# Hybrid attention and convolution layer on one core: key and value projections moved into the query projection's rounds

## The chip, the cores and the metric

The kernel is one launch on one core of a Trainium2 chip. The metric is the device time of that launch in microseconds (us), as a median over runs; lower is better. The core has five engines with their own instruction streams: TensorE (PE, matrix products into the accumulation memory PSUM), VectorE (DVE), ScalarE (ACT), GpSimd (POOL) and SyncE (SP). Here SP issues nearly all transfers; a few small ones are issued by POOL and ACT. Streams run in order, and wait for each other by semaphores.

## The reference

One layer of a diffusion backbone runs over two sets of tokens with the same weights: 128 context tokens and 512 latent tokens, width 1024, float32. Cut to what matters:

```
mod = silu(cond) @ w_ada + b_ada          # shift, scale, gate, twice
h   = rms(x) * norm * (1 + sc1) + sh1
q, k, v, gb, gc, u = split(h @ w_in)      # 512, 128, 128, 512, 512, 512 columns
q = rms_per_head(q); k = rms_per_head(k)  # 8 query heads, 2 key heads, 64 wide
latent q, k get a 2-D rotary position; context q, k do not
attn   = softmax(q k^T / 8) v             # latent: cached keys + latent keys
y_conv = gb * conv3(gc * u)
x = x + g1 * (concat(rms(attn), rms(y_conv)) @ w_out)
x = x + g2 * ((silu(gate) * up) @ w_down) # gate, up from a second normed h
```

The outputs are both sets of tokens after the layer, and the context's keys and values.

## The kernel before

Every matrix product that must be accurate is made of three products of a rounded number type (`mm3`): both operands are split into a rounded high part and the low rest (`split`: ACT copies with rounding, DVE subtracts), and high·high, high·low and low·high are added in PSUM. Tokens stand in five tiles of 128: latent tiles 0 to 3 and the context tile 4 (`CTX`). The contraction over the width of 1024 goes in eight blocks k of 128.

**The first stage** makes h and the query projection. For each k a piece of `w_ada` (two tiles `af` of 512 KB, two transfers each, L323) is multiplied with silu(cond) by `ada1_mm` (step `a`, L379), folded by `ada1_mod` (step `m`, L428) and turned into a scale and a shift by three small DVE operations (L402 to L406). `h_do` (step `h`) applies these to the transposed tokens `xT` and splits the result into `hH[k]` and `hL[k]`. Then five `q_mm` (digits) add block k of the query projection for the five token tiles, three products of 512 columns each, into five PSUM banks that stay open over all eight k. `P1PRE` and `P1SEQ` are written orders of these steps for k = 0 and for the rounds k = 1 to 7. In the first, `r` is a token tile's norm, `x` its transposes, `w` a weight split, `p` and `v` small loads and turns, `c` constants. Under `manual_schedule` PE follows the text's order throughout; DVE, ACT and POOL follow it in `P1PRE` only, and beyond it a scheduler of the framework chooses. `LOADS` is the order in which SP issues the first transfers. The `af` tiles have four buffers and the raw weights `wf` three, so SP waits for their release; split weights `wh` and `wl` have four buffers each.

**The second stage** begins with five evictions of the query projection to SBUF (`qraw`, L549 and L551, tile name `of`), the two transfers of the rotary tables (`act.dma_start`, L561 and L562, issued by ACT), and eight POOL operations on them that make the tables `tab` (L568 and L574). It then follows the written order `SEQ`. Here `k`t is `kv_mm` (L629): 24 products of 256 columns for the keys and values of tile t, then the per-head norm, rotary product and split of the keys (`head_norm`, `k_split`) and the store of the values. `c`/`C` do the same to the cached keys; `K`t turns keys by PE (`k_turn`, L621) and evicts them (L623, L624). `q`t norms and splits a query tile and `Q`t turns it (L657). `a`, `t`, `o` are the three steps of the context's own attention. `S`, `T`, `O` are the scores, transposes and output products of the sixteen latent units (two heads each; `S0.0` is the first). `F1` is a filler: the next third of one half of a convolution's product (`conv_mm`, L677 to L679, 24 products of 320 columns per half) or a piece of the later modulation (`ada_all`). There are 84 fillers (`NFILL`).

The inverse square roots of all norms are POOL operations (`rstd_of`, L164). The third stage (output projection) and the fourth (the FFN) take over half of the time and aren't touched.

Of the kernel before, what the change touches and what calls it, by code (L numbers as in the profile page):

```python
# [9 lines left out]
F32 = mybir.dt.float32  # L10
# [5 lines left out]
P = 128  # L16
# [16 lines left out]
SOQ = [0, -300, -300, -300]  # L33
# [3 lines left out]
XTE = [0, 1, 0, 1, 1, 1, 0, 1, 1, 0]  # L37
SEQ = ('k1 c0 q4 k4 C0 k0 K4 Q4 q0 a0 F1 k2 a1 K0 t0 k3 t1 o0 K1 F1 Q0 o1 K2 F1 K3 F1 S0.0 F1 F1 S0.1 '
# [48 lines left out]
LOADS = [0, 0, 0, 0, 2, 1, -1, 0, 3, 3, 2, 2]  # L87
# [3 lines left out]
def build(ctx, tc, x_prompt, x_sample, c, cache_k, cache_v, c_ctx, norm_mix, norm_ffn, w_ada, b_ada,  # L91
# [144 lines left out]
    def load_split(e, wf):  # L236
# [4 lines left out]
        if gain is None:  # L241
            with early(SOQ[key[1]] if key[0] == 'q' else SOW):
                split(wh, wl, wf)
# [108 lines left out]

    for a in LOADS:
        if a > 0:
            ada1_next(a)
        elif a < 0:
            load_next(True)
        else:
            x_load()
# [53 lines left out]
    def ada1_mm(k):  # L413
# [3 lines left out]
        for h, wf in enumerate(ada1[k]):  # L417
            for i in range(4):
                cond_mm(rp, 4 * h + i, wf[:, i].rearrange("p a b -> p (a b)"))
        res = T("res", (P, 256), F32, 2)  # L420
        dve.tensor_copy(res, rp)
        ada1[k] = res

    def ada1_mod(k):
        res = ada1.pop(k)
        mp = PB((P, 2, 1, 2))
# [5 lines left out]

    def xT_do(t):

        both = PS2() if t < XB else None
        tps = [both[:, i] if t < XB else PB() for i in range(2)]

        def turn(k):
            pe.transpose(tps[k // 4][:, k % 4 * P:(k % 4 + 1) * P], xs[t][:, k * P:(k + 1) * P], ident)

        if t < XB:
            for k in range(KD):
                turn(k)
        for i, tp in enumerate(tps):
            if t >= XB:
                for k in range(4):
                    turn(4 * i + k)
            dst, src = xT[:, 4 * i:4 * i + 4, t * P:(t + 1) * P], tp.rearrange("p (k q) -> p k q", q=P)
            if XTE[2 * t + i] == 0:
                act.activation(dst, src, AF.Copy)  # L450
            else:
                dve.tensor_copy(dst, src)
# [871 lines left out]
```

## Time and profile before

| what | value |
|---|---|
| median of 3 runs | 760.23 us (760.18 to 761.4) |
| the profiled execution's own time | 762.66 us |
| its span, first to last instruction | 760.9 us |
| granted TensorE clock, mean | 0.993 |
| PE busy (modelled ends) | 739.5 us, 97% |
| DVE busy | 552.7 us, 73% |
| ACT busy | 369.6 us, 49% |
| POOL busy | 43.1 us, 6% |
| first query-projection product to last | 20.46 to 65 us |
| first score products of the latent attention | 95.08 us |

In a timeline the first number is an instruction's start in us from the span's start, the second the time that it took; a matrix product's duration includes its way through the array, so that what one costs in a row of many is the distance of two starts. An idle time in square brackets is that of the engine before the instruction, with what ended it. "PEclk" is the granted share of the TensorE clock.

### The profile page before, as it was taken

The numbers are of one execution on the slowest core, as the hardware profiler recorded it, in microseconds if no ns is written. First come the engines' busy times: TensorE is split into PE (matmuls) and PEld (weight loads), VectorE is DVE, ScalarE is ACT, GpSimd is POOL, SyncE is SP. The second block draws the span as 40 slices with busy tenths as digits, with TensorE's granted clock in tenths as the row PEclk, the third lists the DMA queues.
The fourth block names the chain that finished last, engine by engine and source line by source line (L and its number), as shares of the span: only waits on it lengthen the run. The fifth ranks groups of instructions, "written<-read, shape, count | busy, mean of one in ns | idle before, by whom it ended". The sixth has DMA issues, their size and how long they took to land.

```text
span 760.9 us, 11844 instructions
## 1 busy us (share of the span) xinstructions
PE 739.5 (97%) x4580; PEld 664.6 (87%) x4580; DVE 552.7 (73%) x1003; ACT 369.6 (49%) x715; POOL 43.1 (6%) x73
## 2 busy tenths in 40 slices
PE   4999999999999999999999999999999999999997
PEld 3768888989998887899898789998889998899986
DVE  5556987676666797779879678884578866788653
ACT  5345867666656444765552135553125541255410
POOL 3104301011010110100000000000000000000000
PEclk9899999999999999999999999999999999999999
DMA  9985132522433363031335223223113132222312
GB/s 289 293 233 158 38 118 91 173 91 91 160 104 93 130 249 111 1 112 56 86 111 179 83 62 103 79 89 113 53 56 110 58 112 67 73 86 82 111 56 84
DMA packets 102349, 84.52 MB, mean 111 GB/s; under 512 B 4526, under 2 KB 82674, under 8 KB 102292
## 3 DMA queue, kind: packets, MB, share of 16 engines
q1 hardware_dynamic: 100980, 83.39, 35.5%
q8 instruction: 36, 0.59, 0.3%
q10 hardware_dynamic: 1056, 0.26, 0.2%
q0 software_dynamic: 256, 0.11, 0.1%
q14 instruction: 21, 0.17, 0.1%
HBM read 79.68 MB, written 2.75 MB: 108 GB/s over the span
## 4 chain that ended last, share of the span: by engine, by line
PE 82%; DVE 8%; DMA 3%; ACT 2%; SPq 2%; issue 1%; POOL 1%; DVEq 0%; POOLq 0%
PE pf L154 17%; PE pf L156 16%; PE pf L155 16%; PE pc L677 3%; PE pc L678 3%; PE pc L679 3%; PE po L834 3%; PE ps L791 2%; PE ph L154 2%; PE pt L817 2%; PE ph L155 2%; PE ph L156 2%; PE pc L379 2%; DMA af<-in_w_ada_dram 2%; DMA wf<-in_w_gate_up_dram 1%
## 5 line engine op out<-in xcount | busy, mean ns | idle before, releaser
L150 ACT ACTIVATE wh<-wf 128x1024 fp32r<-128x1024 f32 (+1 forms) x76 | 64.1, 843 | 95.7 <-PE pf L156 61.8
L154 PE MATMUL pf<-wh,gT 128*128 128x512 f32 (+1 forms) x225 | 88.1, 392 | 0.0
L155 PE MATMUL pf<-wl,gT 128*128 128x512 f32 (+1 forms) x225 | 87.7, 390 | 0.0
L156 PE MATMUL pf<-wh,gT 128*128 128x512 f32 (+1 forms) x225 | 87.7, 390 | 0.0
L151 DVE TENSOR_TENSOR wl<-wf,wh 128x1024 fp32r<-128x1024 f32 (+1 forms) x42 | 49.4, 1175 | 29.1 <-ACT wh L150 26.3
L677 PE MATMUL pc<-hH,wh 128*128 128x320 f32 x192 | 61.1, 318 | 0.0
L678 PE MATMUL pc<-hL,wh 128*128 128x320 f32 x192 | 59.4, 310 | 0.0
L679 PE MATMUL pc<-hH,wl 128*128 128x320 f32 x192 | 59.4, 309 | 0.0
L155 PEld LDWEIGHTS pf<-wl,gT 128*128 128x128 f32 x225 | 42.2, 188 | 10.0 <-issue 0.2
L154 PEld LDWEIGHTS pf<-wh,gT 128*128 128x128 f32 x225 | 42.2, 188 | 9.9 <-ACT wh L150 0.2
L156 PEld LDWEIGHTS pf<-wh,gT 128*128 128x128 f32 x225 | 42.2, 188 | 9.8
L154 PE MATMUL pf<-T,wh 128*128 128x320 f32 x160 | 49.7, 311 | 0.5 <-ACT u L1154 0.5
L155 PE MATMUL pf<-T,wl 128*128 128x320 f32 x160 | 49.5, 309 | 0.0
L155 PE MATMUL pf<-T,wh 128*128 128x320 f32 x160 | 49.5, 309 | 0.0
L156 PE MATMUL pf<-T,wh 128*128 128x320 f32 x160 | 49.5, 309 | 0.0
L154 PE MATMUL pf<-T,wl 128*128 128x320 f32 x160 | 49.5, 309 | 0.0
L156 PE MATMUL pf<-T,wl 128*128 128x320 f32 x160 | 49.5, 309 | 0.0
L154 PE MATMUL pf<-B,wl 128*128 128x320 f32 x152 | 47.3, 311 | 0.1
L156 PE MATMUL pf<-B,wl 128*128 128x320 f32 x152 | 47.1, 310 | 0.0
L155 PE MATMUL pf<-B,wl 128*128 128x320 f32 x152 | 47.0, 309 | 0.0
L1233 DVE TENSOR_TENSOR dm<-pf,g 128x512 f32<-128x512 f32 (+1 forms) x41 | 27.7, 675 | 22.8 <-PE pf L156 22.6
L154 PE MATMUL pf<-B,wh 128*128 128x320 f32 x136 | 42.3, 311 | 1.5 <-DVE cu L1183 1.5
(293 smaller groups left out, 2023.9 us busy)
## 6 DMA issues: line engine op xcount, KB each, us to landing
wf<-in_w_gate_up_dram SPq DMA_DIRECT2D x44, 512.0 KB, 4.0
aw<-in_w_ada_dram SPq DMA_DIRECT2D x24, 512.0 KB, 4.7
wf<-in_w_down_dram SPq DMA_DIRECT2D x20, 512.0 KB, 3.4
wf<-in_w_in_dram SPq DMA_DIRECT2D x18, 512.0 KB, 6.1
af<-in_w_ada_dram SPq DMA_DIRECT2D x32, 256.0 KB, 6.0
x<-in_x_sample_dram SPq DMA_DIRECT2D x8, 512.0 KB, 4.8
wf<-in_w_out_dram SPq DMA_DIRECT2D x8, 512.0 KB, 3.9
wf<-in_w_ada_dram SPq DMA_DIRECT2D x8, 512.0 KB, 3.7
```

The source lines that it names most:

```text
L150: act.activation(hi, src, AF.Copy)
L151: dve.tensor_tensor(lo, src, f32(hi), ALU.subtract)
L154: pe.matmul(out, lh, rh, start=start, stop=False, skip_group_check=more)
L155: pe.matmul(out, lh, rl, start=False, stop=False, skip_group_check=more)
L156: pe.matmul(out, ll, rh, start=False, stop=stop, skip_group_check=more)
L379: pe.matmul(out[CG * g:CG * (g + 1)], cp[:, k], w, start=(k < 4), stop=(k >= KD - 4), skip_group_check=True)
L677: pe.matmul(acc, wh[:, k], hH[k][:, c0:c0 + n], start=(k == 0), stop=False)
L678: pe.matmul(acc, wh[:, k], hL[k][:, c0:c0 + n], start=False, stop=False)
L679: pe.matmul(acc, wl[:, k], hH[k][:, c0:c0 + n], start=False, stop=(k == KD - 1))
L791: pe.matmul(s2[:, g, :320], q, kk[:, v, P + g * 320:P + (g + 1) * 320], start=(i == 0), stop=(i == 1))
L834: pe.matmul(ov, w, x[:, i].rearrange("p a q -> p (a q)"), start=(g == 0 and i == 0 and n == 0), stop=(last and i == len(kts) - 1 and n == 1))
L1233: dve.tensor_tensor(dm, ps[:, :n], g2[cc][:, oc], ALU.mult)
```

## The change

1. **Keys and values in the rounds.** `kv_mm` is gone. A new step `k` in the first stage (`kv_q`) does block k of the keys and values for the four latent tiles, two token tiles side by side in one PSUM bank, so that two banks stay open over the rounds; the first product into a bank starts it and only the last one ends it. A step `K` (`kv_ctx`) does all eight blocks for the context tile. The three results are evicted to SBUF (`kvctx`, `kvraw`), and the second stage's `k` (`kv_norm`) does only what followed the products.
2. **Loads.** The weights of keys and values are planned between those of the queries, and `LOADS` names all transfers of the stage: `x` a token tile, `A` one k of `w_ada`, `W` the next weights.
3. **Written orders.** One `P1SEQ` covers all rounds, and DVE, ACT, POOL and SP follow the text's order through it as PE does. The steps are cut finer: `r`/`s` (norm and scale), `e` (an eviction of transposes, with its engine), `a`/`b` (products and eviction of the modulation), `w`/`l` (high and low part of a weight). For k = 0 the latent part of h is made without the detour over `hF` on ACT.
4. **Idle products.** `spin` (step `d`) multiplies the identity with itself into a bank that nobody reads: 8, 2 and 4 times.
5. **Second stage.** `SEQ` begins with `k4` and has more fillers ahead of `S0.0` (11 where there were 4) and one fewer in six places behind it; 85 are listed, of which 84 exist as before. The modulation's small PSUM tiles now use the other tag, with one bank left for them beside the context's query sums.

```
-LOADS = [0, 0, 0, 0, 2, 1, -1, 0, 3, 3, 2, 2]
+LOADS = 'xxxxAWxAAWAWAWAWAWAW'
-P1SEQ = 'm h a 0 1 2 3 4'
-P1PRE = ('r0 r1 r2 x0 r3 x1 v0 x2 a0 w0 x3 m0 r4 h00 a1 q02 q01 x4 q00 m1 h01 h10 a2 q03 h11 p0 q04 c0')
+P1SEQ = ('d8 r0 s0 x0 r1 s1 r2 x1 e00d s2 e01d r3 v0 d2 x2 s3 a0 e10d e20a b0 x3 e11d e21a e30a m0 d4 w l h00y q02 r4 q01 e31d s4 '
+         'p0 a1 b1 x4 e40d m1 h01x h10 a2 q00 b2 q03 h11 q04 w l m2 e41a h20 h21 q10 q11 q12 a3 b3 q13 q14 '
+         'm3 h30 h31 q20 q21 w l c0 q22 q23 a4 b4 q24 k0 k1 m4 h40 h41 q30 q31 w l v1 q32 a5 b5 q33 q34 k2 k3 '
+         'm5 h50 h51 q40 q41 w l q42 a6 b6 q43 q44 k4 m6 h60 h61 q50 q51 w l q52 a7 b7 q53 q54 k5 '
+         'm7 h70 h71 q60 q61 q62 q63 q64 k6 K w l k7 q70 q71 q72 q73 q74')
-SEQ = ('k1 c0 q4 k4 C0 k0 K4 Q4 q0 a0 F1 k2 a1 K0 t0 k3 t1 o0 K1 F1 Q0 o1 K2 F1 K3 F1 S0.0 F1 F1 S0.1 '
+SEQ = ('k4 c0 F1 k0 q4 F1 C0 k1 F1 K4 F1 Q4 q0 a0 F1 k2 a1 F1 K0 t0 F1 k3 t1 o0 F1 K1 F1 Q0 o1 K2 F1 K3 F1 '
+       'S0.0 F1 F1 S0.1 q1 F1 F1 S1.0 F1 T0.0 S1.1 T0.1 T0.2 O0.0 F1 O0.1 O0.2 S2.0 T1.0 F1 T1.1 T1.2 S2.1 '
...
-    for j in range(4):
-        plan(("q", j), wi[:, 2 * j:2 * j + 2, O_Q:O_Q + 512])
-    for h in range(2):
-        plan(("kv", h), wi[:, 4 * h:4 * h + 4, O_K:O_K + 256])
+    for x in ("q", 0), ("q", 1), ("kv", 0), ("q", 2), ("kv", 1), ("q", 3):
+        n, o, w = (2, O_Q, 512) if x[0] == "q" else (4, O_K, 256)
+        plan(x, wi[:, n * x[1]:n * x[1] + n, o:o + w])
...
+    pe_order = tc.manual_schedule(engines={mybir.EngineType.PE})
+    pe_order.__enter__()
+    pre_order = tc.manual_schedule(engines={mybir.EngineType.DVE, mybir.EngineType.Activation, mybir.EngineType.Pool,
+                                            mybir.EngineType.SP})
+    pre_order.__enter__()
...
+        if alone and cc == 0:
+            act.activation(hH[k][:, s], xT[:, k, s], AF.Identity, bias=b, scale=a)
+            dve.tensor_scalar(hF[k][:, s], xT[:, k, s], a, b, ALU.mult, ALU.add)
+            dve.tensor_tensor(hL[k][:, s], hF[k][:, s], f32(hH[k][:, s]), ALU.subtract)
+            return
...
+    def spin(n):
+
+        for _ in range(n):
+            pe.matmul(qacc[-1][:, :P], ident, ident, start=True, stop=True)
...
+    def w_hi(_):
+        e, wf = deferred.pop(0)
+        a, b = e[1].shape[1], e[1].shape[2]
+        e[5] = T("wh", (P, a, b), F32R, WHB), T("wl", (P, a, b), F32R, WHB)
+        act.activation(e[5][0], wf, AF.Copy)
+        rounded.append((wf, *e[5]))
...
+    def kv_ctx():
+
+        kvacc.append(PB((P, 256), tag="c"))
+        for k in range(KD):
+            wh, wl = W(("kv", k // 4))
+            mm3(kvacc[2], hH[k][:, 512:TOK], hL[k][:, 512:TOK], wh[:, k % 4], wl[:, k % 4], k == 0, k == KD - 1)
+
+    def kv_q(k):
+
+        if not kvacc:
+            kvacc.extend(PB() for _ in range(2))
+        wh, wl = W(("kv", k // 4))
+        for t in range(NL):
+            s = slice(t * P, (t + 1) * P)
+            out = kvacc[t // 2][:, t % 2 * 256:t % 2 * 256 + 256]
+            first, last = ends("kv%d" % t)
+            mm3(out, hH[k][:, s], hL[k][:, s], wh[:, k % 4], wl[:, k % 4], first and t % 2 == 0, last and t % 2 == 1, True)
...
-    for k in range(1, KD):
-        ada1_next(3)
...
+    kvraw, kvctx = T("g1", (P, 2, 512), F32, 2), T("g1", (P, 256), F32, 2)
+    act.activation(kvctx, kvacc[2], AF.Copy)
+    act.activation(kvraw[:, 0], kvacc[0], AF.Copy)
+    dve.tensor_copy(kvraw[:, 1], kvacc[1])
...
-    def kv_mm(t):
-        acc = PB((P, 256), tag="c")
-        s = slice(t * P, (t + 1) * P)
-        for k in range(KD):
-            wh, wl = W(("kv", k // 4))
-            mm3(acc, hH[k][:, s], hL[k][:, s], wh[:, k % 4], wl[:, k % 4], k == 0, k == KD - 1)
+    def kv_norm(t):
+        acc = kvctx if t == CTX else kvraw[:, t // 2, t % 2 * 256:t % 2 * 256 + 256]
```

More of the change, by code (lines that the diff above doesn't have):

```diff
@@ L241, in load_split @@
         if gain is None:
-            with early(SOQ[key[1]] if key[0] == 'q' else SOW):
+            with early(SOW):
                 split(wh, wl, wf)
@@ L431, in build, with xT_evict, h_do @@
     xT = T("xT", (P, KD, TOK))
+    xps = {}
     def xT_do(t):
         both = PS2() if t < XB else None
[L436 to L441, printed above, removed]
-            for k in range(KD):
[L443 to L452, printed above, removed]
+        xps[t] = [both[:, i] if t < XB else PB() for i in range(2)]
+        for k in range(KD):
+            pe.transpose(xps[t][k // 4][:, k % 4 * P:(k % 4 + 1) * P], xs[t][:, k * P:(k + 1) * P], ident)
+    def xT_evict(t, i, e):
+        dst, src = xT[:, 4 * i:4 * i + 4, t * P:(t + 1) * P], xps[t][i].rearrange("p (k q) -> p k q", q=P)
+        if e == "a":
+            act.activation(dst, src, AF.Copy)
+        else:
+            dve.tensor_copy(dst, src)
     hF = {}
-    def h_do(k, cc):
+    def h_do(k, cc, alone):
         if k not in hF:
@@ L464, in h_do @@
             dve.tensor_scalar(hF[k][:, s], xT[:, k, s], a, b, ALU.mult, ALU.add)
-        if k == 0:
+        if alone:
             split(hH[k][:, s], hL[k][:, s], hF[k][:, s])
@@ L510, in rows2_load @@
         pool.dma_start(rows2[8:20, :], conv_w[0].rearrange("w (r q) -> (w r) q", q=P))
[L512 to L514 removed]
+    steps = {"r": x_norm, "s": x_scale, "c": late_consts, "w": w_hi, "l": w_lo, "p": lambda i: rows2_load(), "x": xT_do,
+             "v": lambda i: (vec_do, vec2_do)[i](), "m": ada1_mod, "a": ada1_mm, "b": ada1_res, "d": spin,
+             "k": kv_q, "K": lambda i: kv_ctx()}
     in_pre[0] = True
[L516 to L517 removed]
+    for x in P1SEQ.split():
+        k = int(x[1:2] or 0)
         if x[0] == "h":
[L519 removed]
+            h_do(k, int(x[2]), len(x) > 3)
         elif x[0] == "q":
             q_mm(k, int(x[2]))
+        elif x[0] == "e":
+            xT_evict(k, int(x[2]), x[3])
         else:
```

63 lines of the change are left out of this document (27 added, 36 removed), and 19 rows, old and new, of the table SEQ.

## The prediction

> **What bounds the kernel now.** I read the windows by stage first, then PE's timeline at the seams, then DVE, ACT and POOL between the two stages. Columns of the windows: busy time and instructions of PE, its weight loads, DVE, ACT, POOL; granted clock; DMA share; GB/s.
>
> ```profile
> 20.00:25.00 5.00, 5.00 (x23) 3.85 (x16) 1.12 (x3) 0.00 (x0) 1.38 (x3) 0.51 1.16 284
> 45.20:65.00 19.80, 19.80 (x115) 15.41 (x115) 9.05 (x21) 7.43 (x10) 1.42 (x2) 1.00 0.75 210
> 65.00:97.00 32.00, 29.81 (x235) 28.06 (x235) 28.43 (x85) 24.38 (x67) 12.57 (x20) 1.00 0.21 64
> 97.00:262.00 165.00, 164.25 (x1183) 148.31 (x1182) 116.05 (x229) 106.85 (x217) 13.91 (x24) 1.00 0.37 118
> 262.00:761.00 499.00, 492.86 (x2844) 449.24 (x2842) 375.35 (x605) 209.04 (x391) 6.74 (x7) 1.00 0.29 92
> ```
>
> From 97 us on PE is full and DVE at 70%: there an instruction taken from PE is time gained, as long as the softmax still finds its cover. From 65 to 97 us DVE is busy 28.4 of 32 us: the norms and splits of keys and queries set the pace, and PE is filled beside them. Before 65 us transfers, waits and a half clock rule. So the products of keys and values leave a stage that DVE bounds, for one in which PE has room.
>
> ```profile
> 12.62 1.16 PE L379 MATMUL pc<-af,cp 128*32 128x256 f32 x16
> 13.72 1.09 PE L439 MATMUL pt<-ident,x 128*128 128x128 f32 x8
> 20.46 0.79 PE L154 MATMUL ps<-wh,hH 128*128 128x512 f32 x1
> 41.57 0.75 PE L379 MATMUL pc<-af,cp 128*32 128x256 f32 x8 [1.52 <-DMA af<-in_w_ada_dram]
> 47.27 0.50 PE L428 MATMUL pt<-sel,res 128*128 128x2 f32 x4
> 47.70 1.07 PE L379 MATMUL pc<-af,cp 128*32 128x256 f32 x16
> 48.70 0.50 PE L154 MATMUL ps<-wh,hH 128*128 128x512 f32 x1
> 52.31 0.50 PE L428 MATMUL pt<-sel,res 128*128 128x2 f32 x4
> 57.35 0.50 PE L428 MATMUL pt<-sel,res 128*128 128x2 f32 x4
> 64.82 0.28 PE L154 MATMUL pc<-wh,hH 128*128 128x256 f32 x1
> 64.94 0.28 PE L155 MATMUL pc<-wl,hH 128*128 128x256 f32 x1
> 78.45 0.31 PE L677 MATMUL pc<-hH,wh 128*128 128x320 f32 x1
> 78.59 0.31 PE L678 MATMUL pc<-hL,wh 128*128 128x320 f32 x1
> 95.08 0.46 PE L791 MATMUL ps<-KA,qT 128*128 128x320 f32 x2
> 129.62 1.72 PE pc L739 x4
> ```
>
> By distance of starts: a `q` round is 52.31 - 48.70 = 3.6 us, `a` 1.0, `m` 0.43, a key product 0.12, a filler product 0.147.
>
> **Rounds, PE.** Five token tiles times 24 products at 0.12 are 14.3 us, now issued before the stage's end. From `a0` at 12.62 on PE has to issue 8 x (3.6 + 1.0 + 0.43) = 40.2, two groups of transposes 2.2, keys and values 14.3, and `d4`: two 512-wide float32 products take 1.72 in the chain, so a 128-wide one 0.21 and four 0.9. Sum 57.6: it ends at 70.2 if nothing waits. `d8` and `d2` (2.1 us by that price) stand where PE waits for x anyway; uncovered, they'd move the start by as much. Waits remain: `q02` needs h of k = 0, whose way (`m0`, weight split, ACT, DVE) ends near 18.5, and the first `w_ada` pieces come at the transfers' pace. Before, PE issued three `q` rounds, five `a`, five `m` and a group of transposes between 14.8 and 42.3, 19.1 us of work in 27.5: 8.4 lost, part of it in the half-clock stretch above. I carry 3 over, since from k = 2 on the rounds last 6 to 10 us with the key products in them, and the same bytes come in that time. So the last q product ends at **73**; the ends are 70.2 and 76 (half clock for 5 us and a wait like that at 41.57).
>
> Three edits of this part I cost at nothing. The 1 MB of key weights goes ahead of the last query weights, with the same bytes before the last `w_ada` piece. SP now issues in the text's order, so a weight whose buffer isn't free holds the `w_ada` pieces queued behind it; the split that frees it runs a round before, and if not, the price is a wait like the 1.52 at 41.57, which the upper end holds. And `a` and `m` share one bank: an `a` right behind an `m` waits for three small DVE operations, about 0.5, which only `m1` and `a2` don't have a round between.
>
> Before, the last product stood at 64.82 with 14.3 to go, 79.1: PE is 6 us ahead.
>
> **The second stage, DVE and POOL.** The products of keys no longer wait there, but the chain behind them stays, and its start isn't at 65.
>
> ```profile
> 59.34 0.74 ACT L150 ACTIVATE hH<-hF 128x640 fp32r<-128x640 f32 x1
> 59.58 0.43 ACTq L561 DMA_DIRECT2D pr<-rope_c_dram  x1
> 60.05 0.51 ACTq L562 DMA_DIRECT2D pr<-rope_s_dram  x1
> 62.20 0.73 POOL L568 TENSOR_TENSOR tab<-pr,gnq 128x256 f32<-128x256 f32 x1 [40.82 <-DMA pr<-rope_c_dram]
> 65.23 1.17 POOL L574 TENSOR_TENSOR tab<-pr,gnq 128x64 f32<-128x64 f32 x4 [1.61 <-DMA pr<-rope_s_dram]
> 66.36 2.15 POOL L574 TENSOR_TENSOR tab<-pr,gnk 128x64 f32<-128x64 f32 x4
> 68.86 0.72 POOL L164 TENSOR_TENSOR rs<-ms,neghalf 128x2 f32<-128x2 f32 x1 [0.36 <-DVE ms L162]
> 65.02 0.69 DVE L549 COPY of<-pc 128x512 f32<-128x512 f32 x1 [3.41 <-PE pc L156]
> 69.95 0.28 DVE L603 TENSOR_TENSOR pr<-pr,rs 128x128 f32<-128x128 f32 x1
> 78.55 1.28 ACT L876 ACT_TABLE_LOAD   x1
> 87.66 1.23 DVE L151 TENSOR_TENSOR wl<-wf,wh 128x1024 fp32r<-128x1024 f32 x1
> 93.23 0.42 DVE L855 TENSOR_TENSOR of<-t,es 64x256 f32<-64x256 f32 x1
> 96.80 0.82 DVE L795 TENSOR_REDUCE nm<-ps 128x1 f32<-128x640 f32 x1
> ...
> 69.95:96.80 26.85, 24.45 (x75) 1.00 0.16 44
> ...
> DVE rs L166 <- POOL rs L164: 1.5, 2, 0.9
> ```
>
> In the changed order the rotary transfers stand on ACT behind hH of k = 7 and the split of the first convolution weight; POOL does all eight table operations ahead of the first key's square root, and DVE's first rotary product waits for all of them. Working back from 73 (`q7` 3.6, `k7` 1.4, `K` 2.9, `k6` 1.4, `q6` 3.6, `m7` 0.4), `m7` stands at 59.7 against 57.35, so the transfers are issued 2.4 later plus up to 1.06 for the split, 62.5. Before, the tables' second part began 5.2 after its issue, with 1 MB of other weights beside it. So the tables end at 62.5 + 5.2 + 1.17 + 2.15 = 71.0, and the root (0.7) at **71.7**; with a landing after 2.6, as the first table had, the products of `K` (68.0) and their eviction bind, and it is 70.
>
> Before, the step that uses the first root stood at 69.95, and S0.0's maximum at 96.80: 26.85 us, 24.45 of them busy (last row but one: DVE alone, in that window; last: its longest wait, for square roots). Now the same work has more in it: 1.1 of steps that stood ahead of that point, the context query's copy 0.6 (at 65.02 before), a third convolution weight's low part 1.15 (L151), a convolution product 0.35, a second pair of L855 and L856 0.9. Busy time so becomes 28.6. Idle between the steps was 2.4. It could be 4.6: in the changed order ACT's table load waits for the first maximum, where it ran beside it (78.55), and two square roots of eight columns are waited for. I take 2.4, as measured. S0.0's maximum comes at 71.7 + 28.6 + 2.4 = 102.7, its products 1.0 earlier (two pairs, 0.6, and their way out), **101.7** against 95.08: **6.6 later**. The ends: no idle and the early tables, 97.6; an idle of 4.6 and 3 us more ahead of it, 107. The evictions of `kvctx` and `kvraw` (ACT twice, DVE once, 0.6 each) run beside `q7`; without that cover they'd add 1.2.
>
> PE has until then: 28.7 us (from 73 to 101.7), with 11 fillers where it had 4 and no key products. It will wait for some 10 us of it; that costs nothing by itself, DVE being the bound.
>
> **Behind S0.0.** 73 fillers are left where there were 80.
>
> ```profile
> L677 PE MATMUL pc<-hH,wh 128*128 128x320 f32 x192 | 61.1, 318 | 0.0
> ```
>
> Three lines of 192 products over 72 fillers are 8 each, x 0.147 = 1.17; seven are **8.2 us** less on a full PE, the work of DVE and ACT that goes with them having moved too. The bound the other way: where a run of fillers loses one, the next unit may wait, up to 1.17 in each of six places. Behind 262 us nothing is touched.
>
> **Sum.** +6.6 - 8.2 = -1.6 on the span of 760.9. The profiled execution took 762.66, 2.4 above the median of 760.23, so I apply the difference to the median: **758.6**.
>
> **The Trainium skill**, TensorE: Matmul & The Clock Gate, Part 1, says that an idle window of about 3.4 us halves PE's clock and one of sustained work restores it. The trace agrees: 0.51 from 20 to 25 us, behind a stretch of waits.
>
> **Rivals.** *The lead survives* (faster). If the chain keeps its 95.08, because the tables land early and all keys being ready lets DVE run without gaps, the 8.2 come out whole: 752; with half of my 6.6, 755. For it: K and V no longer wait for PE. Against it: DVE was busy 28.4 of 32 us already. 754.5.
>
> *The chain slips further* (slower). If the idle is the 4.6 above and the tables come another 2 to 3 us late, S0.0 is 11 to 12 late instead of 6.6: 763.5. It decides against the change from 8.2 on. For it: ACT, DVE and POOL each have one order, in which a split or a table load stands ahead of what the chain needs.
>
> *Lost cover* (slower). Half of six places times 1.17 come back as waits, together with an idle of 3.5: 761.5.
>
> *Half clock in the gap* (slower). PE's waits between 75 and 90 us come in pieces of several us. In the rows of 20 to 25 us the clock stood at 0.51 for 5 us; twice that where PE is on the chain (turns, context scores) costs 2.5 each: 763. By the page's rule this is what a gap over 3.4 us does.
>
> **Chances.** Forecast 0.38 (756.5 to 761.5 by itself: 2.9 lower and 2 more idle at the ends), lead survives 0.27, chain slips 0.20, lost cover 0.07, half clock 0.08. About 0.2%, 1.5 us, is what a measurement can tell from no change. Faster is 0.20 of the forecast and nearly all of the first rival, 0.46; same 0.21; slower 0.33. The range 753 to 765 leaves out the far ends of both sides.
>
> **What would show it.** Right: the last q product at 73 with key products between the rounds; POOL's tables ending near 71; S0.0's products near 102; PE waiting from 75 to 100. Wrong: a clock of 0.5 in the rounds, rounds that wait for `af`, S0.0 before 98 or behind 105, or PE waits between units behind 105.

## The result and the profile after

The changed kernel takes 783.67 us (median of 4 runs, 781.88 to 785.43), the kernel before 760.82 on the same chip: a ratio of 1.0296, 95% interval 1.0265 to 1.0327. It is slower by 22.5 us on 760, far beyond the predicted range. Its profiled execution took 784.24 us, with a span of 782.4 and a mean clock of 0.989.

First the windows by stage, of the changed kernel: the rounds (first to last query product), the head (to the first score products S0.0), the units (to the third stage) and the rest, with some shorter stretches. The columns are those of the prediction.

```profile
16.86:77.64 60.78, 57.01 (x389) 44.40 (x389) 29.43 (x68) 22.43 (x34) 8.44 (x17) 0.97 0.80 222
42.50:50.00 7.50, 5.63 (x34) 4.06 (x33) 2.52 (x4) 0.87 (x1) 0.00 (x0) 0.77 0.71 208
77.88:113.89 36.01, 25.32 (x158) 22.16 (x157) 26.37 (x77) 21.41 (x58) 11.05 (x12) 0.86 0.27 80
85.00:90.00 5.00, 1.35 (x9) 1.09 (x8) 3.47 (x12) 2.46 (x8) 2.79 (x6) 1.00 0.04 12
90.00:95.00 5.00, 3.78 (x18) 3.51 (x19) 3.81 (x15) 2.91 (x7) 3.18 (x2) 0.54 0.00 0
74.50:117.40 42.90, 30.87 (x184) 26.50 (x183) 30.84 (x89) 24.29 (x67) 14.43 (x21) 0.88 0.29 83
78.30:117.40 39.10, 27.07 (x167) 23.37 (x166) 29.02 (x83) 22.67 (x62) 10.67 (x11) 0.87 0.26 76
113.89:279.10 165.21, 158.26 (x1122) 141.37 (x1120) 113.79 (x230) 104.00 (x214) 10.27 (x23) 0.99 0.34 106
279.10:782.40 503.30, 497.18 (x2861) 452.98 (x2861) 376.96 (x607) 210.64 (x395) 8.36 (x9) 1.00 0.30 91
```

And the windows of the kernel before that answer to them: rounds, head, the stretch from DVE's first norm step to the first maximum, and the units; ahead of them, two windows of its early part.

```profile
14.80:20.46 5.66, 2.35 (x21) 0.94 (x20) 4.38 (x10) 3.61 (x6) 2.62 (x5) 0.79 1.17 296
14.80:42.30 27.50, 22.67 (x156) 15.72 (x155) 15.97 (x43) 12.84 (x18) 3.54 (x6) 0.87 1.07 292
20.46:65.00 44.54, 43.02 (x259) 32.51 (x256) 21.95 (x56) 17.80 (x23) 2.35 (x4) 0.91 0.92 256
65.00:95.08 30.08, 27.89 (x222) 26.14 (x221) 26.51 (x82) 24.38 (x67) 12.57 (x20) 1.00 0.21 64
68.20:96.80 28.60, 26.41 (x206) 24.66 (x206) 26.18 (x82) 21.20 (x61) 9.60 (x14) 1.00 0.18 52
95.08:257.69 162.61, 161.86 (x1177) 146.74 (x1176) 113.66 (x227) 102.54 (x207) 11.67 (x22) 1.00 0.38 119
```

The rounds last 61 us instead of 44.5, and begin 3.6 earlier. The head lasts 36 instead of 30 with PE busy 25 of them, although the key products are gone from it. The units show 55 products fewer and last 2.6 us longer: PE is busy 158.3 of 165.2, where it was full. (The very first product of S0.0 goes 1.6 us ahead of the others here. Counted from S0.0's maximum, at 117.40 against 96.80, it is 20.6 us late and the units are 0.8 longer.) S0.0 is 18.8 us late, the third stage begins 21.4 late (279.10 against 257.69), and behind it nothing has changed.

Then the timeline of the changed kernel, row by row along that path.

```profile
42.51 0.40 PE L157 MATMUL ps<-wh,hL 128*128 128x512 f32 x1
43.41 1.22 DVE L530 TENSOR_TENSOR wl<-wf,wh 128x1024 fp32r<-128x1024 f32 x1
44.55 0.17 DVE L555 COPY vec<-pc 128x20 f32<-128x20 f32 x1
44.77 1.07 PE L384 MATMUL pc<-af,cp 128*32 128x256 f32 x16 [1.87 <-DVE vec L555]
66.94 0.49 ACTq L606 DMA_DIRECT2D pr<-rope_c_dram  x1
72.74 0.73 POOL L613 TENSOR_TENSOR tab<-pr,gnq 128x256 f32<-128x256 f32 x1 [50.44 <-DMA pr<-rope_c_dram]
76.43 1.16 POOL L619 TENSOR_TENSOR tab<-pr,gnk 128x64 f32<-128x64 f32 x4
77.64 0.40 PE L157 MATMUL pc<-wh,hL 128*128 128x512 f32 x1
78.30 0.29 DVE L648 TENSOR_TENSOR pr<-pr,rs 128x128 f32<-128x128 f32 x1 [1.99 <-POOL rs L165]
81.93 0.69 DVE L594 COPY of<-pc 128x512 f32<-128x512 f32 x1
88.09 0.17 DVE L167 TENSOR_SCALAR rs<-rs 128x8 f32<-128x8 f32 x1 [1.53 <-POOL rs L165]
91.20 1.39 PE L698 MATMUL pt<-identr,qT 128*128 128x128 f32 x8 [4.85 <-DVE qT L690]
96.44 1.28 ACT L917 ACT_TABLE_LOAD   x1 [1.90 <-DVE nm L915]
97.73 0.37 ACT L917 ACTIVATE pr<-ps,nm 128x128 f32<-128x128 f32 x1
102.80 1.23 DVE L152 TENSOR_TENSOR wl<-wf,wh 128x1024 fp32r<-128x1024 f32 x1 [1.36 <-ACT wh L151]
111.74 0.17 DVE L167 TENSOR_SCALAR rs<-rs 128x8 f32<-128x8 f32 x1 [1.53 <-POOL rs L165]
113.25 0.42 DVE L896 TENSOR_TENSOR of<-t,es 64x256 f32<-64x256 f32 x1 [1.33 <-DMA es<-t]
113.89 0.31 PE L832 MATMUL ps<-KA,qT 128*128 128x320 f32 x1
277.82 0.39 PE L875 MATMUL po<-pl,VS 128*128 128x256 f32 x1 [0.58 <-DVE pl L152]
279.10 0.50 PE L155 MATMUL ph<-wh,m 128*128 128x512 f32 x1 [0.89 <-ACT rs L773]
```

At 42.5 PE stands: the products `a5` need the one PSUM bank that `v1` holds until DVE has copied it out (L555), and DVE does a weight's low part first. The clock is 0.77 over the 7.5 us from there. The rotary transfers are issued at 66.9, the tables end at 77.6 (they are ten POOL operations, two of L613 and eight of L619, and not the eight named above), and DVE uses the first square root at 78.3. From there to the first maximum DVE waits again and again, six times for 1.2 to 1.5 us: three times for a root, twice for ACT, once for a transfer. In the stretch from its first norm step (74.5) to that maximum (117.4) it is busy 30.8 us of 42.9; before, 26.2 of 28.6.

### The profile page after: what moved, and what is told of

The parts are those of the page before. It is cut to its first block, busy times and chain, and to the rows that moved or that the text cites. A ratio compares the mean times of both kernels' runs of the same rounds, so it can differ in the third digit from the quotient of the medians.

```text
span 782.4 us, 11922 instructions
## 1 busy us (share of the span) xinstructions
PE 749.8 (96%) x4608; PEld 670.9 (86%) x4608; DVE 555.2 (71%) x1005; ACT 368.3 (47%) x716; POOL 43.3 (6%) x73
## 3 DMA queue, kind: packets, MB, share of 16 engines
q1 hardware_dynamic: 100980, 83.39, 34.9%
## 5 line engine op out<-in xcount | busy, mean ns | idle before, releaser
L151 ACT ACTIVATE wh<-wf 128x512 fp32r<-128x512 f32 (+1 forms) x69 | 56.5, 819 | 87.1 <-PE pf L157 62.0
L152 DVE TENSOR_TENSOR wl<-wf,wh 128x1024 fp32r<-128x1024 f32 (+1 forms) x35 | 41.2, 1176 | 30.3 <-ACT wh L151 27.4
```

The costliest lines, as they stand in the source:

```text
L151: act.activation(hi, src, AF.Copy)
L152: dve.tensor_tensor(lo, src, f32(hi), ALU.subtract)
```

## The experiments

"Rounds end" is the start of the last query product, "units" the time from S0.0 to the third stage; both, and S0.0, are from one profiled execution each. The ratio is to the kernel before, with its 95% interval.

| run | ratio | rounds end | S0.0 | units |
|---|---|---|---|---|
| before | 1 | 64.59 | 95.08 | 162.6 |
| changed | 1.0296 [1.0265, 1.0327] | 77.64 | 113.89 | 165.2 |
| v1 later | 1.0253 [1.0217, 1.0289] | 74.97 | 111.38 | 165.4 |
| tables early | 1.0288 [1.0268, 1.0307] | 79.71 | 114.53 | 162.7 |
| old filler places | 1.0265 [1.0240, 1.0289] | 76.42 | 109.69 | 163.7 |
| exp table early | 1.0277 [1.0259, 1.0296] | 77.96 | 114.20 | 162.2 |
| context query first | 1.0258 [1.0238, 1.0277] | 76.42 | 111.85 | 162.0 |
| context behind | 1.0359 [1.0341, 1.0377] | 78.42 | 102.92 | 180.0 |
| keys last | 1.0244 [1.0224, 1.0264] | 71.70 | 112.39 | 160.2 |
| three together | 1.0209 [1.0194, 1.0225] | 75.03 | 105.17 | 164.8 |
| roots covered | 1.0224 [1.0200, 1.0248] | 76.61 | 107.40 | 165.0 |
| queries normed under keys | 1.0190 [1.0165, 1.0216] | 70.18 | 105.20 | 163.9 |
| no idle products | 1.0288 [1.0262, 1.0315] | 78.59 | 115.11 | 162.7 |
| before, new second stage | 1.0096 [1.0074, 1.0117] | 61.31 | 99.28 | 162.7 |
| keys left behind | 1.0074 [1.0053, 1.0095] | 63.15 | 96.39 | 163.5 |
| and v1 later | 1.0037 [1.0025, 1.0049] | 61.94 | 94.42 | 163.5 |
| and tables early | 1.0018 [1.0007, 1.0030] | 61.82 | 92.30 | 164.3 |
| and context's keys in | 1.0125 [1.0106, 1.0144] | 66.34 | 97.98 | 166.4 |
| before, tables early | 1.0028 [1.0016, 1.0039] | 62.58 | 93.17 | 162.7 |

The executions differ in the early part: with the same rounds, "before" ends them at 64.59 and "before, new second stage" at 61.31. That is the execution of before on which the prediction was built, 2.4 us above its median. So the ratios decide, and the positions show where.

My theory from these rows was a late and slow head: rounds that stall, tables that come late, and steps that wait for each other in one order. The rival was lost cover behind S0.0. The first four runs take one suspect each.

**v1 later.**

```
- ... q30 q31 w l v1 q32 a5 b5 ...   m7 h70 h71 ...
+ ... q30 q31 w l q32 a5 b5 ...      m7 v1 h70 h71 ...
```

> One edit: the step v1 (turn of the last small rows, and its copy by DVE) goes from the round of k = 4 to behind m7. In the changed kernel the products a5 wait for that copy (one PSUM bank is left for a, m and v1), PE stands for 1.9 us at 42.5 us and the granted clock is 0.66 from 45 to 50. Theory 'stalled rounds': the last q product comes 3 to 4 us earlier (74 instead of 77.9), the rotary transfers with it (63.5 instead of 66.9), and as the chain behind is serial, the first score products and the whole kernel too: 780 instead of 783.7. Rival 'the w_ada pieces bind the rounds': PE stands at the next piece instead, less than 1 us is gained, 783.

```profile
42.76 1.07 PE L384 MATMUL pc<-af,cp 128*32 128x256 f32 x16
42.50:50.00 7.50, 7.50 (x59) 6.11 (x58) 3.12 (x7) 2.02 (x4) 0.00 (x0) 1.00 1.03 291
```

`a5` starts 2.0 earlier without a wait, PE is full and the clock 1.00 in the same 7.5 us. The rounds end 2.7 earlier and S0.0 comes 2.5 earlier. The stall was real and worth some 2.7 us in the trace, a little less than expected; the transfers don't take its place. The intervals of the two ratios overlap, so that the medians alone wouldn't show it.

**Tables early.**

```
+ a step t: act.dma_start of both tables into a tile of their own, and POOL's ten operations
- 'm5 h50 h51 ...
+ 't m5 h50 h51 ...
```

> One edit: the two rotary transfers and POOL's eight table operations stand in the text ahead of m5 instead of behind the last product (with a tile of their own for the transfers). Theory 'the tables are late': the first square root of a key follows the eviction of the context's keys (73.2 us) instead of the tables (77.6), so DVE's first rotary step stands at about 74.5 instead of 78.3, and S0.0 and the end move by the same 3.8: 780. Rival 'the head is slow in itself' (DVE, ACT and POOL wait for each other in their one order, whatever the start): the start moves and S0.0 by less than 1 us, 783.

The tables end at 51.8 instead of 77.6, and DVE uses the first root at 77.54 instead of 78.30, with rounds that end 2.1 later. Behind the last query product that is 2.8 earlier, and S0.0 still comes 34.8 behind that product (changed: 36.3). The tables alone don't hold the head. Of the 2.1, 1.2 stood there before the edit could act (first query product at 18.11 against 16.86); what made the rest isn't settled.

**Exponential's table early.**

```
- ... w l k7 q70 ...
+ ... w l k7 E q70 ...      # E: act.activation(warm, warm, AF.Exp)
```

> One edit: ACT does one exponential on a single column ahead of the products of k = 7, so that the table load of 1.28 us (at 96.4 us, behind the first maximum of the context's scores) is made where ACT has time. Theory 'the head is one serial chain': 1.3 us less for S0.0 and the end, 782.4. Rival 'the context's own attention is beside the chain of the keys': no change, 783.7.

The load stands at 68.65, beside PE's products, and S0.0 at 114.20: no gain there. The ratio's interval overlaps with that of the changed kernel.

**Old filler places**, and the other way round, **the kernel before with the new second stage.**

```
- SEQ = 'k4 c0 F1 k0 q4 F1 C0 k1 F1 K4 F1 Q4 q0 a0 F1 k2 a1 F1 K0 t0 F1 k3 t1 o0 F1 K1 F1 Q0 o1 K2 F1 K3 F1 S0.0 ...'    # 73 fillers behind S0.0
+ SEQ = 'k4 c0 k0 q4 C0 k1 K4 Q4 q0 a0 F1 k2 a1 K0 t0 k3 t1 o0 K1 F1 Q0 o1 K2 F1 K3 F1 S0.0 ...'    # 80 fillers behind S0.0, as before
```

> One edit: the steps ahead of S0.0 keep the new order but have the old four fillers, and from S0.0 on the order is the one before, with all its fillers (80 behind S0.0 where there were 73). Theory 'lost cover': behind S0.0 the seven fillers bring 8 us of products back, and the 10 us that PE lost there between the units go, while the head is no slower: 780 to 784, about the same. Rival 'the waits behind S0.0 are not for want of fillers': the 8 us come on top, 791; and if the fillers ahead of S0.0 slowed the head by their weight splits and evictions, the head gets shorter by 3 to 5.

```
- SEQ of the kernel before
+ SEQ of the changed kernel     # nothing else in the kernel before
```

> The kernel before, with nothing but the new order of the second stage: k4 first, 11 fillers ahead of S0.0 instead of 4, one fewer in six places behind. Theory 'fillers are cover behind S0.0 and cost ahead of it': S0.0 later by 4 to 8 us (seven times 1.17 on a PE that lost only 4.7 us there), and from S0.0 to the third stage no gain worth more than 2: 763 to 768. The prediction's own rule (a filler behind S0.0 is 1.17 us of a full PE, ahead of it it fills waits): S0.0 later by 3.5 at most and 8.2 gained behind: 755.

The units of the first and of the second of these runs, and the second's head:

```profile
109.69:273.36 163.67, 161.63 (x1177) 146.46 (x1176) 111.67 (x223) 102.59 (x207) 11.16 (x22) 1.00 0.36 114
```

```profile
99.28:262.00 162.72, 157.42 (x1122) 141.31 (x1121) 111.44 (x225) 101.81 (x207) 9.68 (x22) 0.99 0.33 105
65.00:99.28 34.28, 31.98 (x251) 29.99 (x250) 27.68 (x84) 22.69 (x63) 11.02 (x14) 1.00 0.35 104
```

With 1177 products or with 1122 the units last the same: 162.6 and 162.7 in the kernel before, 163.7 and 165.2 in the changed one. Over all runs but that with the context behind, the units last 160.2 to 165.4 us with the new places and 162.6 to 166.4 with the old ones, so the 8 us didn't come out; a gain of 1 or 2 can't be told from this scatter. What the seven fillers leave behind is idle time of PE (in the kernel before 161.9 busy against 157.4). Ahead of S0.0 they don't seem to be free: in the kernel before, S0.0 comes 38.0 behind the last query product instead of 30.5, and the kernel is slower by 0.96% (7.3 us), though this run also has the keys' order of the new text (k4 first), which wasn't tried apart; in the changed kernel, taking them back brings S0.0 4.2 forward, 3.0 of it in the head; of the 5.7 that this execution gains by the third stage the medians keep 2.4, with intervals that overlap. So the seven fillers behind S0.0, taken together, were cover.

**Where the head hangs.** Two runs test whether it is on the context query, whose sums DVE copies out at 81.9, behind other work.

```
- ... k7 q70 q71 q72 q73 q74
+ ... k7 q74 y4 q70 q71 q72 q73             # y4: the copy out, in the text's order
```

> One edit: in the last round the context tile's query products (q74) come ahead of those of the four latent tiles, and DVE copies their sums out right behind, in the text's order; in the changed kernel that copy is made at 81.9 us, 4 us behind the last product, with a weight's low part and other copies ahead of it. Theory 'the chain hangs on the context query' (copy, square, root, turn, the context's scores, which all stand on PE ahead of the latent keys' turns): from that copy to S0.0 it was 30.1 us in the kernel before and 32.0 in the changed one; the copy comes at about 76, so S0.0 comes 5 to 6 earlier (108 to 109), and the end too: 778. Rival 'the chain hangs on the keys' (tables, first root at 78.3): S0.0 moves by less than 1.5 us, 783.

```
- ... q63 q64 k6 K w l k7 q70 q71 q72 q73 q74
+ ... q63 q64 w l q74 y4 q70 y0 q71 q72 q73 K k6 k7
```

> One edit of the last round: the key products that stood ahead of q7 (k6, K, k7; 5.7 us of PE) go behind it, the context's query first, and the sums of the context's and the first latent query are copied out in the text's order. If the chain hangs on the context query, its copy comes at 70 to 71 us instead of 81.9, PE has the key products to do beside the query's norm, and S0.0 comes 7 to 10 earlier (104 to 107): 775. If it hangs on the keys, whose evictions now come 4 to 5 us later (78 instead of 73.2), S0.0 comes no earlier, or up to 4 later: 783 to 788.

The copy comes at 75.10 in the first and at 68.38 in the second, 6.8 and 13.5 us earlier, and S0.0 only 2.0 and 1.5 earlier. The theory of the context query falls. From the last product of the rounds, keys or queries, to S0.0 it is 35.4 and 34.9 (77.49 is the last key product of the second), so S0.0 keeps its distance from whatever product comes last. By its ratio the second run is nonetheless faster than the changed kernel, by 0.5% or 4.0 us, with intervals that just don't touch: its units last 160.2, 5 less, for a reason that isn't settled.

```
- SEQ = 'k4 c0 F1 k0 q4 ... Q4 q0 a0 ... t1 o0 ... S0.0 ...'
+ SEQ = 'c0 F1 k0 F1 C0 k1 F1 q0 F1 k2 F1 K0 F1 k3 F1 K1 F1 Q0 F1 K2 F1 K3 F1 S0.0 k4 F1 F1 S0.1 q4 ... a0 ... o1 ...'
```

> One edit of the order of the second stage: the context tile's key, query and attention steps (k4 K4 q4 Q4 a t o) go behind S0.0, into the first latent units; 11 fillers stay ahead of S0.0. If the chain hangs on the context query, S0.0 waits only for the latent keys and the first latent query and comes 8 to 12 us earlier (102 to 106); the context's 9 us of DVE work move into the units, where PE is full, so part of it comes back: 774 to 779. Rival 'the chain hangs on the keys': S0.0 moves by 3 us at most, 781 to 784.

```profile
102.92:282.87 179.95, 166.82 (x1162) 148.47 (x1160) 121.97 (x248) 112.32 (x239) 12.14 (x24) 0.97 0.31 98
```

S0.0 comes 11 us earlier, as expected, and the units last 14.7 longer: PE has 13.1 us without work there. The expected 774 to 779 us became 787. So it isn't the moment at which the context's sums are copied out that holds S0.0, but the context's steps do take some 11 us of the head; they are paid wherever they stand, and among the units they cost more.

**Mending what was found.**

```
  v1 behind m7  +  q74 y4 first  +  old filler places
```

> Three edits together: v1 behind m7 (2.5 us earlier S0.0 by its run alone), the old filler places (S0.0 4.2 earlier, and 1.5 less from S0.0 to the third stage), and the context's query first (5 to 6 if the chain hangs on it). If they add up, S0.0 comes at 102 and the kernel takes 771; if the chain hangs on something that all three share, no better than the best of them alone, 778 to 780.

```
  the same, with SEQ = 'q4 k4 c0 k0 C0 k1 Q4 K4 q0 a0 ...' and q1 behind T0.2
```

> The run with three edits, and the second stage's text changed so that q4 comes ahead of k4 and q1 three steps later, which puts other DVE steps between a square root's operand and its use. Of the 7.0 us that DVE idled there, 4.6 were three waits of 1.53 for roots of eight columns. If they are on the chain, idle falls to 3 or 4 us, q1's 1.5 us of work leave the head, and S0.0 comes 4 to 5 earlier: 771 instead of 775.3. Rival 'other waits take their place' (turns on PE, ACT): 774 to 776.

```
  v1 behind m7; t ahead of m7; ... q64 w l q74 y4 q70 y0 q71 q72 q73 K k6 k7
  SEQ = 'q4 k4 c0 q0 k0 C0 Q4 K4 k1 a0 ...', old filler places, q1 behind T0.2
```

> Several edits together, to see whether the reading of the head can be turned into time: v1 behind m7; the rotary transfers and tables ahead of m7; the last round's queries ahead of its keys (as in the run with the keys last); the old filler places; and in the second stage q4 and q0 ahead of the latent keys, q1 three steps later. Reading: time to S0.0 is the start of DVE's norm work, plus its busy time, plus its idle time between serial steps (before 68.2 + 26.2 + 2.4, changed 74.5 + 30.9 + 12.1, the run with three edits 71.4 + 27.6 + 7.0). Here the queries' norms can begin at 69 to 70 beneath the key products, so idle falls to 3 or 4 and S0.0's maximum comes at 98 to 101: 765 to 768. Rival 'the queue of keys behind the last product is what counts': S0.0 no earlier than with the three edits (105), 775.

DVE's stretch from its first norm step to S0.0's maximum, in the first and in the last of the three:

```profile
71.40:106.00 34.60, 22.56 (x127) 19.75 (x126) 27.57 (x86) 23.40 (x66) 12.20 (x12) 0.80 0.19 55
```

```profile
68.94:105.99 37.05, 26.45 (x163) 23.91 (x162) 26.59 (x79) 23.99 (x66) 8.74 (x11) 0.77 0.25 70
```

The three edits bring 6.6 us of the 22.5 by their ratios, half of what was hoped. Covering the roots brings nothing (its interval overlaps with that of the three edits, from above). Starting DVE's norms 2.5 us earlier, at 68.9, doesn't move S0.0 at all: DVE idles 10.5 us instead of 7.0. The reading "start plus busy plus idle" describes the head but doesn't predict it, since what is taken from one of its waits comes back in another.

**No idle products.**

```
- 'd8 r0 ...   v0 d2 x2 ...   m0 d4 w l ...
+ 'r0 ...      v0 x2 ...      m0 w l ...
```

> The changed kernel without the idle products (d8, d2 and d4). If they only stand in waits, nothing changes (783, first query product at 17, clock the same). If they keep the clock up, the first products of the modulation and of the query run at half the clock without them: first query product 1 to 3 us later, S0.0 and the end with it, 785 to 787. If they are in the way, 1 us faster.

Ratio 1.0288 against 1.0296, first query product at 17.57 against 16.86: the idle products make no difference that these runs can tell (in runs that have them the first query product comes anywhere from 16.77 to 18.11).

**The core taken out.** The key products go back to the second stage, tile by tile; the new first stage stays.

```
- for x in ("q", 0), ("q", 1), ("kv", 0), ("q", 2), ("kv", 1), ("q", 3):
+ for x in ("q", 0), ("q", 1), ("q", 2), ("q", 3), ("kv", 0), ("kv", 1):
- ... k0 k1 ... k2 k3 ... k4 ... k5 ... k6 K w l k7 ...      # kv_norm
+ (none of them)                                             # kv_mm and SEQ as before
```

> The changed kernel without its core: the keys and values are projected in the second stage, token tile by token tile, as before (order of the second stage as before, weights of the keys behind those of the queries); the loads, the written orders, the finer steps and the idle products of the first stage stay, the wait at v1 too. Theory 'the core of the change is the loss: 14.3 us of key products went from a stretch where PE had them beside DVE's norms into rounds that PE bounds, and what came in pieces now comes at once, so DVE idles': the last query product comes 12 to 15 us earlier than in the changed kernel (63 to 66 against 77.6), from it to S0.0 it is 30 us again as before (36.3 in the changed kernel), DVE idles 2 to 4 us there instead of 12.1, S0.0 at 93 to 96: 758 to 761. Rival 'the first stage's new form is the loss' (written orders on DVE, ACT and SP, one PSUM bank for a, m and v1): the head stays at 35 us and more after the last query product, S0.0 beyond 98, 764 or more.

```
+ v1 behind m7, as above
```

> As the run with the keys left behind, and v1 behind m7. In the changed kernel that edit alone brought S0.0 2.5 us forward. If the rounds without key products still wait there: last query product at 61 to 63, S0.0 at 91 to 93, 755 to 758, faster than the kernel before. Rival 'the transfers bind the rounds without key products' (those rounds have 14.3 us less on PE for the same bytes): PE waits for the pieces of w_ada instead, no gain over the run without this edit.

```
+ v1 behind m7, and the step t (rotary transfers and tables) ahead of m7
```

> As the run before this one (keys left behind, v1 later), with the rotary transfers and tables ahead of m7. In the kernel before the first root's use stood at 69.95, 1.5 behind the end of the tables (68.5). If the tables hold the head where the keys come in pieces, S0.0 comes 1 to 3 us earlier than without this edit: 753 to 757. If not (in the changed kernel this edit alone moved S0.0 by +0.6), no gain, or the transfers delay w_ada's pieces and it is 1 to 2 slower.

Of the run with the keys left behind: the windows of its rounds, of its head (to S0.0) and of DVE's stretch, and from the timeline its last query product and S0.0. Then windows of rounds and head, and rows, of the run with the old filler places, which has the same first stage but for the keys in it (and takes k4 first behind it):

```profile
16.77:63.15 46.38, 41.85 (x269) 28.78 (x269) 25.93 (x62) 18.43 (x25) 3.54 (x6) 1.00 0.98 271
63.15:96.39 33.24, 29.21 (x223) 27.74 (x222) 27.27 (x82) 24.32 (x67) 13.90 (x22) 0.95 0.19 52
66.80:98.10 31.30, 27.27 (x206) 25.85 (x205) 26.61 (x83) 21.10 (x61) 11.64 (x21) 0.95 0.17 48
63.15 0.40 PE L157 MATMUL pc<-wh,hL 128*128 128x512 f32 x1
96.39 0.46 PE L832 MATMUL ps<-KA,qT 128*128 128x320 f32 x2
```

```profile
16.83:76.42 59.59, 55.47 (x388) 43.21 (x389) 31.27 (x79) 23.25 (x37) 9.03 (x18) 1.00 0.82 227
76.42:109.69 33.27, 17.57 (x104) 16.14 (x103) 24.95 (x69) 20.40 (x57) 9.14 (x10) 0.74 0.15 42
76.42 0.39 PE L157 MATMUL pc<-wh,hL 128*128 128x512 f32 x1
109.69 0.46 PE L832 MATMUL ps<-KA,qT 128*128 128x320 f32 x2
```

This is the pair that settles it. The clock is 1.00 in both rounds, and PE is without work 4.5 us (46.38 - 41.85) in the one and 4.1 in the other: the key products (14.3 us by the prediction's price, 13.6 of PE's busy time here, 55.47 - 41.85) filled 0.4 us of waits and made the rounds 13.2 longer. From the last query product to S0.0 it is 33.2 us with the key products in that stretch (96.39 - 63.15) and 33.3 without (109.69 - 76.42): taking them out of the head gained nothing. That is a net reading, since the head without them has PE busy for 17.6 us only and a clock of 0.74 against 0.95, and takes the keys in another order. The expectation was half right: rounds and S0.0 stand near where the theory put them, but the head isn't the 30 us of the kernel before; the core's cost lies in the rounds. By the ratios the core alone is 1.0265 - 1.0074, 1.9% or 14.5 us of the 22.5; the new form of the first stage is 0.74%, 5.6 us, and the fillers' move what remains, 2.4, within its intervals. Another pair agrees on the core: three edits together against the keys left behind with v1 later, 1.0209 - 1.0037, is 1.7%.

Of those 5.6, v1 is 2.8 (1.0074 to 1.0037), and the tables 1.4 more, though there the intervals overlap. What is left, 1.0018, is slower than the kernel before by 0.2%, at the limit of what can be told. The rounds end then at 61.8, where the kernel before ended them at 61.3 in the run with the new second stage: the written orders, finer steps and idle products gained no time that shows. Both runs had been expected to be faster than the kernel before, at 755 to 758 and 753 to 757.

**One piece put back**, and the tables' edit in the kernel before.

```
- ... q63 q64 w l q70 ...
+ ... q63 q64 K Y w l q70 ...     # K: context tile's 24 products; Y: act.activation(kvctx, ...); SEQ = 'k4 c0 k1 q4 C0 K4 k0 Q4 ...'
```

> The run with the keys left behind, v1 later and the tables early, and one piece of the change put back: the context tile's keys and values alone (step K, 24 products, 2.9 us) are projected in the last round, ahead of q7, and evicted there, so that DVE can begin its norms beneath q7; the second stage begins with k4. If the head is DVE's norm work from its start on: the first root's use comes at 63 to 65 instead of 67.2 and S0.0 at 89 to 91 instead of 92.3, 758 to 760. Rival 'what goes into a round is paid in full by PE': q7 and the latent keys behind it come 2.9 later, S0.0 at 92 to 95, 761 to 764.

```profile
63.27 0.39 ACT L543 ACTIVATE g<-pc 128x256 f32<-128x256 f32 x1 [4.86 <-PE pc L157]
63.55 1.05 ACT L523 ACTIVATE wh<-wf 128x1024 fp32r<-128x1024 f32 x1
64.64 1.23 DVE L530 TENSOR_TENSOR wl<-wf,wh 128x1024 fp32r<-128x1024 f32 x1 [0.66 <-ACT wh L523]
65.78 0.28 DVE L635 TENSOR_REDUCE hq_ss<-ph 128x2 f32<-128x128 f32 x1
67.17 0.29 DVE L652 TENSOR_TENSOR pr<-pr,rs 128x128 f32<-128x128 f32 x1 [0.83 <-POOL rs L165]
97.98 0.45 PE L840 MATMUL ps<-KA,qT 128*128 128x320 f32 x2
```

The rival was right and too mild. The context's keys are in SBUF at 63.7, but ACT and DVE split the next weight first, as the text has it, and the first root is used at 67.17, where it was without the edit (67.21). The rounds end 4.5 later (0.5 of it a later first product), S0.0 comes 5.7 later, and the kernel is slower by 1.07% (1.0125 against 1.0018), 8.1 us for 2.9 us of products. What adds to the 2.9 isn't settled.

```
+ rope_tabs() at k == 6 in the loop over the rounds     # in the kernel before: both transfers and the ten table operations
```

> The kernel before with the rotary transfers and tables early (ahead of the sixth round in the text; nothing else): in it DVE's first rotary product waits for the tables, which end at 68.5, and the first root is used at 69.95, 5 us behind the last query product. If they hold the head: S0.0 1 to 2 us earlier, 758 to 759 against 760.2. If the keys' products hold it (first ones end at 67.9): no change; if the 256 KB delay the first tokens: up to 1 slower.

Slower by 0.28%, and S0.0, at 93.17, stands 30.6 behind the last query product, as before (30.5): it isn't the tables that hold the kernel before. No version tried beats it.

## Why the prediction was wrong

The forecast was the sum 6.6 later at S0.0 less 8.2 behind it; by the traces it was 18.8 later and 2.6 more. In the forecast's own terms the last query product came 4.6 later than forecast, S0.0 followed it after 36.2 us instead of 28.7, and the stretch behind S0.0 was 10.8 longer than forecast. Two steps failed: "the products leave a stage that DVE bounds, for one in which PE has room", and "seven are 8.2 us less on a full PE". Besides them DVE's idle time ahead of S0.0, taken as 2.4, was mis-sized. Point by point:

- *Rounds, PE: the last q product at 73.* 77.64, outside the ends of 70.2 and 76. With v1 later it is 74.97, 2 us off. That this is so near is in part luck: without key products these rounds end at 61.94, 2.4 earlier than the sum would have it with all its 8.4 of waits (64.3), and the key products add 13.0 to them where 8.9 were forecast. The rest of the miss is the stall, under "three edits at nothing": the shared bank was priced at 0.5 and only for `m1`/`a2`. The step that holds the bank longest is `v1`, whose copy stands on DVE behind a weight's low part of 1.22. Its price was 2.7.
- *"I carry 3 over", 5.4 of 8.4 us of waits filled by key products.* Measured 0.4. Of the 8.4, PE was without work for only 4.8 (27.50 - 22.67, in the window from 14.80 to 42.30 of the kernel before), 3.3 of that ahead of the first query product, where no key product can stand; most of the rest is the slower clock (0.87 over the stretch). The new rounds without keys run at 1.00, and the 4.5 us of waits in them aren't filled by key products either. This is the first step that failed: "the products leave a stage that DVE bounds, for one in which PE has room". They left a stage where they cost nothing that shows, for rounds in which 13.2 us were paid for them. The sentence "PE is 6 us ahead" compares PE's end with its end before, where it wasn't on the path.
- *The first root at 71.7.* 78.30. The transfers were issued 4.4 later than assumed (66.94), with the rounds; they landed 5.8 behind that, as taken (5.2), and the ten table operations, all still to do then, took 4.9 instead of the 3.3 that the sum had for the last of them. But the tables, early, moved S0.0 by +0.6: the chain worked out from them wasn't the one that holds the head.
- *From the root to S0.0 30.0, with 28.6 busy and 2.4 idle to its maximum.* 35.6, and 39.1 to the maximum, with DVE busy 29.0, as forecast, and 10.1 idle: the idle time is the term that was mis-sized. Both rivals' words on this were right in kind ("a split or a table load stands ahead of what the chain needs"; 4.6 of idle), and too small. That the idle time was small before because keys came one tile at a time is argued, not shown; from the last query product to S0.0 DVE idles 6.0 us with the keys left behind and 8.3 with the old filler places, over the same 33 us, so the idle time isn't a cost by itself. 11 fillers ahead of S0.0 were costed as free of PE time ("PE will wait for some 10 us of it"); by the two filler runs seven of them lengthen the head by 3.0 and 7.5, the second with the keys' new order in it.
- *Behind S0.0, -8.2.* This is the second step that failed. The products did go: 55 rows fewer, six fillers of 1.17 and a group of the modulation of 1.0, 8.0 us. None of it came out as time: 162.6 and 162.7 us in the kernel before. "Up to 1.17 in each of six places" was named as the bound the other way, and the rival *lost cover* took half of it; the run on the kernel before shows the whole of it. What argued for it was in the quoted window: PE was full there, but full with work put in to fill waits of a chain that runs beside it. Busy isn't bound.
- *Half clock in the gap.* It came: 0.54 from 90 to 95 us, behind a gap of 4.85 before the row at 91.20, in a 5 us window with 1.35 of PE work. The Trainium skill, TensorE: Matmul & The Clock Gate, Part 1, has an idle window of about 3.4 us halve the clock, and the trace agrees. In the kernel before the agreement is looser than the prediction has it: from 14.8 us on no single wait of PE ahead of the 0.51 was longer than 1.2 us, with PE busy 2.35 of 5.66. What the half clock cost by itself wasn't tried; the run with three edits has 0.80 over DVE's stretch, and S0.0 as close behind its last product (30.1) as the kernel before with 1.00 (30.5), which speaks for little.
- *What would show it wrong* did: S0.0 behind 105, waits between the units.

What stays open is why the head needs some 30 us from the last product of the rounds on, whatever its order: the edits moved single waits in it, and none, with the context's attention left in it, brought it below 29.2 (75.98 to 105.20, queries normed under keys).

## What to carry to other kernels

Before moving work off a stage, ask whether it costs anything there: 14.3 us of products in a head that lasts 33 us with or without them were free, and in rounds that PE bounds they were paid nearly whole, 13.2 us. A full engine is no proof that its work is the bound: where the order was filled by hand, take a filler out alone and see whether the stretch gets shorter. And where several steps are put on one buffer, price the step that holds it longest, with all that stands ahead of its release on the releasing engine.

## What the runs showed of the hardware that wasn't expected

- ACT's table load took 1.28 us, and the first exponential started 1.29 behind its start (the rows at 96.44 and 97.73). The Trainium skill, ScalarE: Activation LUTs, What ACT_TABLE_LOAD costs, gives 2.66 with a drain; here only the load shows, also where ACT was busy right up to it (exponential's table early: load at 68.65, next operation at 69.94). Moved beside PE's products, it gained S0.0 nothing (114.20 against 113.89).

- The same rounds took 44.1 us in the kernel before and 40.8 in its run with the new second stage, with the clock at 0.51 and 0.73 from 20 to 25 us and PE busy 43.0 and 40.2. A position early in one trace is good to some 3 us, and a prediction anchored on it carries that.
